# adaLN products in fp32 on four column tiles, and key transposes of 128 columns, in a two-layer hybrid mixer on Trainium2

## The chip, the core and the metric

The kernel runs on one core of a Trainium2 chip. The metric is the device time of one execution, in microseconds (us). The core's engines are called by their names or by the profile's: TensorE (PE; its weight loads are PEld), VectorE (DVE), ScalarE (ACT), GpSimd (POOL), SyncE (SP, whose queue issues most of the DMAs). Each engine works through its own instructions in order.

## What is computed

Two layers, each one mixer with post-normalisation, over 2048 latent tokens (`x`) and 256 context tokens (`ctx`) of width 1024:

```python
shift, scale, gate = split(silu(c) @ w_ada + b_ada, 3)        # (1024) @ (1024 x 3072), per layer
shift_c, scale_c, gate_c = split(silu(c_ctx) @ w_ada + b_ada, 3)
z  = (x  * (1 + scale)   + shift)   @ w_in                    # 1024 x 2560
zc = (xc * (1 + scale_c) + shift_c) @ w_in
# z is cut into: gated MLP over chunks of 128 tokens, grouped-query attention
# (8 heads, 2 key heads, RMS norm and rotary), bidirectional RG-LRU
y = concat(mix_a * silu(a_g), attn * silu(b_g), lru * silu(r_g)) @ w_o
x_new = layer_norm(alpha * x + gate * y)
```

The change touches the first two lines (called adaLN below) and the way in which the keys are laid out for the attention's scores.

## The kernel before

Most products are made in fp16 pairs: a float32 operand is scaled and written as a high part and a low part (the rest), and three products hh, hl, lh are summed in PSUM. The program has a start (`ada_start`, L96), and then for each layer a projection stage (`z_phase`, L299) and an attention stage (`att_phase`, L826).

*The start.* `ada_start` makes shift and scale of layer 0, for both `c` and `ctx` (two rows). The 1024 x 2048 columns of `w_ada` come in 16 chunks of 128 x 1024 (`wada`, six buffers, L113). `split` (L133) turns each into `wadh` on ScalarE (L137) and `wadl` on VectorE (L138). The stationary operand is `vs`, 128 x 4: the high and low parts of silu(c) and silu(c_ctx). Four products per chunk (L157, L158, 512 columns each) add into `acc`, which has four rows: high and low parts. `row` (L123) scales them and adds the bias, and `turn` (L127) turns them with eight float32 products with `sel`, which also adds high and low, into columns `adaT`. The order of TensorE, SyncE, ScalarE and VectorE is as written there.

*The rest of adaLN.* Gate of layer 0, and gate, scale and shift of layer 1, are made by a generator, `ada_rest` (L333), beside layer 0's projections, from the second token block on. An item is one chunk of 128 x 512: a load into `wga` (a buffer of the tag `xm`, which `prep` uses as well), the conversion on ScalarE (L384) and VectorE (L385) into the single buffer `wgh`, and at the next visit two products into `gtp` (L376, L377; `gtp` is one of four buffers of the tag `zps`, which the projections use too). After eight items the row is scaled and added to the bias (L379); `fin` (L351) then either turns it (`gtr`, L355) or adds its halves with a product (`gsu`, L359) and stores the gate to DRAM (L361). `pump(rest, 1)` visits the generator once in each section of 24 products: in `nat` at k = 4 (L537), 512 columns each, and in `conv_in` at k = 4 (L686), 256 columns each. A full block of 256 tokens has eight `nat` and four `conv_in` sections, so 12 visits.

*The projections.* `z_phase` goes over nine blocks (L799). In each, the sections rx, rg, ag, kv, uv, bg run in this order (L807). Generators for normalisation and heads (`heads`, L582), gated MLP (`gmlp`), recurrence (`lru`) and the next block's transposes (`prep`) are advanced by `tick` between the sections. Only TensorE's order is written out here (L782); the other engines' instructions are put in order by the framework, and each engine then works in that order.

*The keys.* `heads` gets the reciprocal roots `rs` with a GpSimd power (L588), scales the heads on VectorE (L596), and writes `kc`, 128 tokens x (high, high, low) x 64 per key head (L624, L625). Four transposes follow per 128 tokens: for each of two key heads one of 128 columns (high, high; L641) and one of 64 (low; L642). ScalarE copies them to `KK` (L643) and `KB` (L644, its first 64 rows). The query transposes `qp` (L648), eight per 128 tokens, are all of 128 columns.

*The attention.* Scores, exponentials and values go in a fixed order on all engines but SyncE (L1284).

## Time and profile before

| | |
|---|---|
| runs | 2929.77, 2930.40, 2931.66 us, median 2930.4 us |
| the profiled execution | 2929.47 us, its span (first to last instruction) 2927.7 us |
| PE busy | 2734.7 us, 93% of the span |
| DVE, ACT, POOL busy | 70%, 48%, 61% |
| mean granted TensorE clock | 0.979 |

Busy time of PE is the union of its matmuls, whose ends are modelled, so the space between the starts of neighbours is the better measure of what one costs. The last column of a timeline row tells how long the engine stood idle before the instruction and which instruction released it. Stages: the start to about 37 us, layer 0's projections to about 700 us, its attention to about 1500 us, and the same for layer 1 behind.

### The profile page before, as it was taken

To read this page: it belongs to the slowest core of one execution; us is meant where nothing else is said; L and a number is where in the kernel's file an instruction comes from. 1 tells how busy PE (TensorE), PEld (TensorE's weight loads), DVE (VectorE), ACT (ScalarE), POOL (GpSimd) and SP (SyncE) were. 2 spreads that over 40 slices of the span, in tenths; PEclk is the share of its full clock that TensorE was granted. 3 is DMA by queue.
4 is the path that set the end of the run, shared out by engine and by line. 5 is a ranking of instruction groups with operands and counts; after the bars stand their busy time and mean duration, and the time that the engine had idled before them with its cause. 6 is when DMAs were issued, how large, how long until landed. Compare 5 with 4: busy or idle time off the path is not lost. (4 is left out here: it accounts for less than half of the span.)

```text
span 2927.7 us, 60696 instructions
## 1 busy us (share of the span) xinstructions
PE 2734.7 (93%) x23931; PEld 1821.0 (62%) x23931; DVE 2062.4 (70%) x4102; ACT 1402.3 (48%) x2594; POOL 1784.0 (61%) x1821
## 2 busy tenths in 40 slices
PE   7999999989799999999999899998988999999998
PEld 3544444546677777677765555564566777777775
DVE  7666565567988777777877555554798877777775
ACT  5444444536554445445542454444465544544452
POOL 3233333356888877677764244433498877887775
PEclk9999999999999999999999999999999999999999
DMA  8222222105421110212114111111433210111001
GB/s 289 85 92 93 86 92 78 53 28 178 131 77 58 56 41 27 69 37 70 52 34 158 52 56 54 50 64 38 140 105 99 70 47 24 49 48 42 26 27 44
DMA packets 118254, 213.60 MB, mean 73 GB/s; under 512 B 13872, under 2 KB 45428, under 8 KB 117968
## 3 DMA queue, kind: packets, MB, share of 16 engines
q1 hardware_dynamic: 115620, 208.84, 21.2%
q8 instruction: 187, 3.06, 0.4%
q10 hardware_dynamic: 2348, 0.89, 0.1%
q14 instruction: 99, 0.81, 0.1%
HBM read 147.54 MB, written 62.14 MB: 72 GB/s over the span
## 5 line engine op out<-in xcount | busy, mean ns | idle before, releaser
L1070 POOL TENSOR_TENSOR Pl<-P 128x512 f16<-128x512 f32 x1131 | 1223.4, 1100 | 329.4 <-ACT P L1063 322.0
L1063 ACT ACTIVATE P<-stp 128x512 f32<-128x512 f32 x1160 | 693.1, 598 | 781.6 <-PE stp L1060 701.0
L978 DVE TENSOR_REDUCE pm<-sps 128x1 f32<-128x256 f32 (+1 forms) x1276 | 750.6, 626 | 270.3 <-PE sps L976 267.6
L1060 PE MATMUL stp<-aQB,KB 65*128 65x256 f16 x2320 | 580.0, 275 | 1.6 <-ACT aQB L991 1.6
L1059 PE MATMUL stp<-aQS,KK 128*128 128x256 f16 x2320 | 577.3, 274 | 0.0
L1087 PE MATMUL pv<-VX,P 128*128 128x129 f16 x4640 | 561.1, 220 | 0.0
L1089 PE MATMUL pv<-VX,Pl 128*128 128x65 f16 x4640 | 529.1, 193 | 6.1 <-POOL Pl L1070 3.1
L976 PE MATMUL sps<-KK,aQS 128*128 128x256 f16 (+1 forms) x1276 | 457.7, 360 | 60.1 <-DVE pm L978 57.4
L1089 PEld LDWEIGHTS <-Pl 128*128 128x128 f16 x4640 | 416.9, 98 | 99.8 <-POOL Pl L1070 5.1
L1087 PEld LDWEIGHTS <-P 128*128 128x128 bf16 x4640 | 431.4, 98 | 64.6 <-issue 49.8
L1060 PEld LDWEIGHTS <-KB 65*128 65x128 f16 x2320 | 227.8, 98 | 91.2 <-issue 0.5
L1059 PEld LDWEIGHTS <-KK 128*128 128x128 f16 x2320 | 230.1, 99 | 83.2 <-issue 13.9
L520 POOL TENSOR_SCALAR xh<-xm 128x512 f16<-128x512 f32 x68 | 46.5, 683 | 276.1 <-ACT xm L517 275.4
L531 PEld LDWEIGHTS <-xh 128*128 128x128 f16 x1040 | 103.1, 99 | 152.7 <-issue 50.8
L533 PEld LDWEIGHTS <-xl 128*128 128x128 f16 x1040 | 103.1, 99 | 125.1 <-issue 7.2
L532 PEld LDWEIGHTS <-xh 128*128 128x128 f16 x1040 | 103.0, 99 | 108.6 <-issue 5.9
L682 PE MATMUL cps<-xh,wh_cc 128*128 128x256 f16 x528 | 147.7, 280 | 4.1 <-POOL xh L520 4.1
L683 PE MATMUL cps<-xl,wh_cc 128*128 128x256 f16 x528 | 147.4, 279 | 3.1 <-DVE xl L521 3.1
L684 PE MATMUL cps<-xh,wl_cc 128*128 128x256 f16 x528 | 147.3, 279 | 1.7 <-DVE wl_cc L185 1.7
L433 POOL TENSOR_SCALAR gt<-gt,sp 128x256 f32<-128x256 f32 x72 | 44.1, 622 | 159.9 <-ACT gt L430 153.9
L976 PEld LDWEIGHTS <-aQS 128*128 128x128 f16 x1276 | 124.8, 98 | 9.7 <-DVE yB L1110 0.4
L755 ACT ACTIVATE uv<-uv 128x512 f32<-128x512 f32 x34 | 21.4, 630 | 204.4 <-DVE uv L754 204.4
(284 smaller groups left out, 5581.4 us busy)
## 6 DMA issues: line engine op xcount, KB each, us to landing
wf<-in_w_in_dram SPq DMA_DIRECT2D x64, 256.0 KB
wga<-in_w_ada_dram SPq DMA_DIRECT2D x64, 256.0 KB
lr<-LRd SPq DMA_DIRECT2D x32, 512.0 KB
SBd<-sbg SPq DMA_DIRECT2D x34, 256.0 KB
QSd<-QS SPq DMA_DIRECT2D x17, 512.0 KB
LRd<-gt SPq DMA_DIRECT2D x34, 256.0 KB
aQS<-QSd SPq DMA_DIRECT2D x17, 512.0 KB
asb<-SBd SPq DMA_DIRECT2D x17, 512.0 KB
```

What stands on the lines that cost most here:

```text
L531: T.matmul(ps[:, :w], xh[:, k, ts], wh[:, k, c0:], start=(k == 0), stop=False)
L682: T.matmul(ps, wh[:, k, cs], xh[:, k], start=(k == 0), stop=False)
L683: T.matmul(ps, wh[:, k, cs], xl[:, k], start=False, stop=False)
L684: T.matmul(ps, wl[:, k, cs], xh[:, k], start=False, stop=(k == KC - 1))
L976: T.matmul(ps[:, :w], QS[:, h, t * 128:(t + 1) * 128], KK[:, kv].rearrange("p a b -> p (a b)")[:, k0:k0 + w], start=True, stop=True)
L978: V.tensor_reduce(pm[:, i:i + 1], ps[:, :w], axis=AX, op=OP.max)
L1059: T.matmul(ps[:, i], KK[:, kv, kt], QS[:, h], start=True, stop=False)
L1060: T.matmul(ps[:, i], KB[:, kv, kt], QB[:, h], start=False, stop=True)
L1063: S.activation(P, ps, AF.Exp)
L1070: less_busy(0.6, 1.04, 2.0).tensor_tensor(Pl, P, Ph, op=OP.subtract)
L1087: T.matmul(pv[:, t, 0:129], Ph[:, i, ts], VX[:, kt, kv, 0:129], start=first, stop=False, skip_group_check=True)
L1089: T.matmul(pv[:, t, 64:129], Pl[:, i, ts], VX[:, kt, kv, 64:129], start=False, stop=end, skip_group_check=True)
```

## The change

`vs` becomes float32, 128 x 2. In the start, the products are made in float32 from the loaded chunk itself. The accumulator is 128 x 256: column group g of 256 goes to rows 32g and 32g + 1, so that each of the four products per chunk sits on column tile g of the array. A product of zeros opens each accumulation. The bias is added by one operation over all 128 rows, and the turning takes rows 32g, 32g + 1 with columns of the identity. `wada` has eight buffers.

In `ada_rest`, the items are chunks of 128 x 1024 (32 in place of 64), with one buffer `wga` of their own and no conversion. The generator yields four times per item, `nat` visits it at k = 1 and k = 5, and `conv_in` at k = 4 as before. Gates are stored from rows 32g, four stores each; `gsu` is gone.

In `heads`, `kc` is laid out (low, high, high), and the second transpose of a key head takes (low, high), 128 columns; `KB` still takes the first 64 rows.

```diff
--- before.py
+++ after.py
@@ -69,8 +69,7 @@
     idF = cst.tile([128, 128], F32, name="idF")
     idH = cst.tile([128, 128], F16, name="idH")
     nhalf = cst.tile([128, 32], F32, name="nhalf")
-    vs = cst.tile([128, KC, 4], F16, name="vs")
-    sel = cst.tile([4, 2], F32, name="sel")
+    vs = cst.tile([128, KC, 2], F32, name="vs")
     adaT = [[cst.tile([128, KC, 2], F32, name=f"adaT{l}{j}") for j in range(2)] for l in range(DEPTH)]
     gate_d = [dr.tile([2, D], F32, name=f"gate_d{l}") for l in range(DEPTH)]
     x1_d = dr.tile([SEQ, D], F32, name="x1_d")
@@ -100,73 +99,47 @@
             nc.scalar.dma_start(craw[8:16], c_ctx.rearrange("(k p) -> k p", p=128))
             bts = []
             for j in range(2):
-                bt = p.tile([4, D], F32, name=f"bt{j}")
+                bt = p.tile([128, 256], F32, name=f"bt{j}")
                 V.memset(bt, 0.0)
-                nc.scalar.dma_start(bt[0:2], rows_bcast(b_ada[0, j * D:(j + 1) * D], D, 2))
+                for g in range(4):
+                    c0 = j * D + g * 256
+                    nc.scalar.dma_start(bt[32 * g:32 * g + 2], rows_bcast(b_ada[0, c0:c0 + 256], 256, 2))
                 bts.append(bt)
             iot = p.tile([128, 128], I32, name="iot")
             G.iota(iot, pattern=[[1, 128]], base=0, channel_multiplier=-1)
             V.tensor_scalar(idF, iot, 0.0, None, op0=OP.is_equal)
-            V.tensor_tensor(sel, idF[0:4, 0:2], idF[0:4, 2:4], op=OP.add)
-            ws, tps = [], []
+            zer = p.tile([128, 256], F16, name="zer")
+            V.memset(zer, 0.0)
+            ws = []
 
             def load():
                 j, k = len(ws) // KC, len(ws) % KC
-                ws.append(p.tile([128, D], F32, name="wada", tag="wada", bufs=6))
+                ws.append(p.tile([128, D], F32, name="wada", tag="wada", bufs=8))
                 nc.sync.dma_start(ws[-1], w_ada[0, k * 128:(k + 1) * 128, j * D:(j + 1) * D])
 
-            for _ in range(6):
+            for _ in range(8):
                 load()
-            accs = [pp.tile([4, 2, 512], F32, name=f"acc{j}") for j in range(2)]
-            rows = [bt.rearrange("p (a b) -> p a b", b=512) for bt in bts]
-
-            def row(j, n):
-                V.scalar_tensor_tensor(rows[j][:, n], accs[j][:, n], 1.0 / (CS * WS), rows[j][:, n],
-                                       op0=OP.mult, op1=OP.add)
-
-            def turn(j):
-                tp = pp.tile([128, KC, 2], F32, name=f"tp{j}")
-                for k in range(KC):
-                    T.matmul(tp[:, k], rows[j][:, k // 4, k % 4 * 128:(k % 4 + 1) * 128], sel, start=True, stop=True)
-                tps.append(tp)
-
-            def split(i):
-                w = ws[i].rearrange("p (a b) -> p a b", b=512)
-                wh = p.tile([128, 2, 512], F16, name="wadh", tag="wadh", bufs=3)
-                wl = p.tile([128, 2, 512], F16, name="wadl", tag="wadl", bufs=3)
-                S.activation(wh, w, AF.Copy, scale=WS)
-                V.scalar_tensor_tensor(wl, w, WS, wh, op0=OP.mult, op1=OP.subtract)
-                if len(ws) < 2 * KC:
-                    load()
-                return wh, wl
-
-            parts = [split(0)]
             S.activation(craw, craw, AF.Silu)
             cps = pp.tile([128, 2, KC], F32, name="cps")
             T.transpose(cps.rearrange("p i k -> p (i k)"), craw, idF[:16, :16])
-            vcs = p.tile([128, KC, 2], F32, name="vcs")
-            V.tensor_copy(vcs, cps.rearrange("p i k -> p k i"))
-            V.tensor_scalar(vs[:, :, 0:2], vcs, CS, None, op0=OP.mult)
-            V.scalar_tensor_tensor(vs[:, :, 2:4], vcs, CS, vs[:, :, 0:2], op0=OP.mult, op1=OP.subtract)
-            for i in range(2 * KC):
-                j, k = i // KC, i % KC
-                if i + 1 < 2 * KC:
-                    parts.append(split(i + 1))
-                wh, wl = parts.pop(0)
-                for n in range(2):
-                    T.matmul(accs[j][:, n], vs[:, k], wh[:, n], start=(k == 0), stop=False)
-                    T.matmul(accs[j][:, n], vs[:, k], wl[:, n], start=False, stop=(k == KC - 1))
-                if i == KC + 1:
-                    row(0, 0)
-                    row(0, 1)
-                if i == KC + 3:
-                    turn(0)
-                if i == KC + 5:
-                    V.tensor_scalar(adaT[0][0], tps[0], 0.0, None, op0=OP.add)
-            row(1, 0)
-            row(1, 1)
-            turn(1)
-            V.tensor_scalar(adaT[0][1], tps[1], 1.0, None, op0=OP.add)
+            V.tensor_copy(vs, cps.rearrange("p i k -> p k i"))
+            tps = []
+            for j in range(2):
+                acc = pp.tile([128, 256], F32, name=f"acc{j}")
+                T.matmul(acc, zer[:, 0:128], zer, start=True, stop=False, skip_group_check=True)
+                for k in range(KC):
+                    w = ws[j * KC + k]
+                    for g in range(4):
+                        T.matmul(acc[32 * g:32 * g + 2], vs[:, k], w[:, g * 256:(g + 1) * 256], start=False,
+                                 stop=(k == KC - 1), skip_group_check=True)
+                    if len(ws) < 2 * KC:
+                        load()
+                V.tensor_tensor(bts[j], acc, bts[j], op=OP.add)
+                tp = pp.tile([128, KC, 2], F32, name=f"tp{j}")
+                for k in range(KC):
+                    T.matmul(tp[:, k], bts[j][:, k % 2 * 128:(k % 2 + 1) * 128],
+                             idF[:, 32 * (k // 2):32 * (k // 2) + 2], start=True, stop=True)
+                V.tensor_scalar(adaT[0][j], tp, float(j), None, op0=OP.add)
 
     GRP = {"uv": (0, 512), "ag": (512, 512), "kv": (1024, 512), "bg": (1536, 512), "cc": (2048, 512)}
 
@@ -305,7 +278,7 @@
             def pop(i):
                 return st.enter_context(tc.tile_pool(name=f"zps{l}_{i}", bufs=1, space=PSUM, reuse_waits="tile"))
 
-            zp = Router(op, ["wh_ag wl_ag wh_kv wl_kv wh_uv wl_uv", "xn xm xh xl wgh grow",
+            zp = Router(op, ["wh_ag wl_ag wh_kv wl_kv wh_uv wl_uv", "xn xm xh xl wga grow",
                              "rx qk t1 t2 kc qc QS rp ct sn uv vhl ss rs rt mv s6 rv rsq2 sag sbg zm",
                              "wh_bg wl_bg gt0 gt1 lra th xr xrh xrl hc"])
             pp = Router(pop, ["zc", "tr", "zps"])
@@ -331,63 +304,54 @@
                 return early.pop(0)
 
             def ada_rest():
-                items = [(l2, j, h, k) for l2, j in [(0, 2)] + [(a, b) for a in range(1, DEPTH) for b in (2, 1, 0)]
-                         for h in range(2) for k in range(KC)]
-                ws, parts, acc, row, fins = [], [], None, None, None
+                items = [(l2, j, k) for l2, j in [(0, 2)] + [(a, b) for a in range(1, DEPTH) for b in (2, 1, 0)]
+                         for k in range(KC)]
+                zer = MZ[1][:, 0, 0:1].to_broadcast([128, 128])
+                mov = MZ[2][:, 0:1, 0:64].to_broadcast([128, 4, 64])
+                ws, acc, row, fins = [], None, None, None
 
                 def ld(i):
-                    l2, j, h, k = items[i]
-                    ws.append(zp.tile([128, 512], F32, name="wga", tag="xm", bufs=2))
-                    c0 = j * D + h * 512
-                    nc.sync.dma_start(ws[-1], w_ada[l2, k * 128:(k + 1) * 128, c0:c0 + 512])
-
-                def bias(l2, j, h):
-                    row = zp.tile([4, 512], F32, name="grow", tag="grow")
-                    V.memset(row, 0.0)
-                    c0 = j * D + h * 512
-                    nc.sync.dma_start(row[0:2], rows_bcast(b_ada[l2, c0:c0 + 512], 512, 2))
-                    return row
-
-                def fin(l2, j, h, row):
+                    l2, j, k = items[i]
+                    ws.append(zp.tile([128, D], F32, name="wga", tag="wga"))
+                    nc.sync.dma_start(ws[-1], w_ada[l2, k * 128:(k + 1) * 128, j * D:(j + 1) * D])
+
+                def fin(l2, j, row):
                     if j < 2:
-                        tp = pp.tile([128, 4, 2], F32, name="gtr", tag="tr", bufs=2)
-                        for k in range(4):
-                            T.matmul(tp[:, k], row[:, k * 128:(k + 1) * 128], sel, start=True, stop=True)
-                        V.tensor_scalar(adaT[l2][j][:, 4 * h:4 * h + 4], tp, float(j), None, op0=OP.add)
+                        tp = pp.tile([128, KC, 2], F32, name="gtr", tag="tr", bufs=2)
+                        for k in range(KC):
+                            T.matmul(tp[:, k], row[:, k % 2 * 128:(k % 2 + 1) * 128],
+                                     idF[:, 32 * (k // 2):32 * (k // 2) + 2], start=True, stop=True)
+                        V.tensor_scalar(adaT[l2][j], tp, float(j), None, op0=OP.add)
                     else:
-                        ps = pp.tile([2, 512], F32, name="gsu", tag="tr", bufs=2)
-                        T.matmul(ps, sel, row, start=True, stop=True)
-                        V.tensor_copy(row[0:2], ps)
-                        nc.sync.dma_start(gate_d[l2][:, h * 512:(h + 1) * 512], row[0:2])
+                        for g in range(4):
+                            nc.sync.dma_start(gate_d[l2][:, g * 256:(g + 1) * 256], row[32 * g:32 * g + 2])
 
                 ld(0)
                 yield
-                for i in range(len(items) + 1):
+                yield
+                for i, (l2, j, k) in enumerate(items):
+                    if k == 0:
+                        acc = pp.tile([128, 256], F32, name="gtp", tag="zps", bufs=4)
+                        T.matmul(acc, zer, mov, start=True, stop=False, skip_group_check=True)
+                        row = zp.tile([128, 256], F32, name="grow", tag="grow")
+                        G.memset(row, 0.0)
+                        for g in range(4):
+                            c0 = j * D + g * 256
+                            nc.sync.dma_start(row[32 * g:32 * g + 2], rows_bcast(b_ada[l2, c0:c0 + 256], 256, 2))
+                    w = ws.pop(0)
+                    for g in range(4):
+                        T.matmul(acc[32 * g:32 * g + 2], vs[:, k], w[:, g * 256:(g + 1) * 256], start=False,
+                                 stop=(k == KC - 1), skip_group_check=True)
+                    if i + 1 < len(items):
+                        ld(i + 1)
+                    if k == KC - 1:
+                        V.tensor_tensor(row, acc, row, op=OP.add)
+                        fins = l2, j, row
+                    for _ in range(4):
+                        yield
                     if fins:
                         fin(*fins)
                         fins = None
-                    if i:
-                        l2, j, h, k = items[i - 1]
-                        w = parts.pop(0)
-                        if k == 0:
-                            acc = pp.tile([4, 512], F32, name="gtp", tag="zps", bufs=4)
-                        if k == 2:
-                            row = bias(l2, j, h)
-                        T.matmul(acc, vs[:, k], w[:, 0], start=(k == 0), stop=False)
-                        T.matmul(acc, vs[:, k], w[:, 1], start=False, stop=(k == KC - 1))
-                        if k == KC - 1:
-                            V.scalar_tensor_tensor(row, acc, 1.0 / (CS * WS), row, op0=OP.mult, op1=OP.add)
-                            fins = l2, j, h, row
-                    if i < len(items):
-                        w = zp.tile([128, 2, 512], F16, name="wgh", tag="wgh")
-                        f = ws.pop(0)
-                        S.activation(w[:, 0], f, AF.Copy, scale=WS)
-                        V.scalar_tensor_tensor(w[:, 1], f, WS, w[:, 0], op0=OP.mult, op1=OP.subtract)
-                        parts.append(w)
-                        if i + 1 < len(items):
-                            ld(i + 1)
-                    yield
-                fin(*fins)
 
             W = Wt[l]
 
@@ -533,7 +497,7 @@
                     T.matmul(ps[:, :w], xl[:, k, ts], wh[:, k, c0:], start=False, stop=(k == KC - 1))
                     if t:
                         pump(fm, 1)
-                    if k == 4:
+                    if k % 4 == 1:
                         pump(rest, 1)
                 return ps
 
@@ -621,8 +585,8 @@
                                                 snv[:, None, :, s].to_broadcast([128, w, 2, 16]), op=OP.mult)
                         V.tensor_tensor(t1, t1, t2, op=OP.add)
                     kc = zp.tile([128, 2, 3, 64], F16, name="kc", tag="kc", bufs=2)
-                    V.tensor_copy(kc[:, :, 0:2], t1[:, 8:10, None].to_broadcast([128, 2, 2, 64]))
-                    V.tensor_tensor(kc[:, :, 2], t1[:, 8:10], kc[:, :, 0], op=OP.subtract)
+                    V.tensor_copy(kc[:, :, 1:3], t1[:, 8:10, None].to_broadcast([128, 2, 2, 64]))
+                    V.tensor_tensor(kc[:, :, 0], t1[:, 8:10], kc[:, :, 1], op=OP.subtract)
                     kcs.append(kc)
                     if full(b):
                         qc = zp.tile([128, 8, 2, 64], F16, name="qc", tag="qc", bufs=2)
@@ -638,8 +602,8 @@
                     kc = kcs[t]
                     kp = pp.tile([128, 2, 2, 128], F16, name="kp", tag="tr", bufs=2)
                     for j in range(2):
-                        T.transpose(kp[:, 0, j], kc[:, j, 0:2].rearrange("p a b -> p (a b)"), idH)
-                        T.transpose(kp[0:64, 1, j], kc[:, j, 2], idH)
+                        T.transpose(kp[:, 0, j], kc[:, j, 1:3].rearrange("p a b -> p (a b)"), idH)
+                        T.transpose(kp[:, 1, j], kc[:, j, 0:2].rearrange("p a b -> p (a b)"), idH)
                     S.copy(KK[:, :, kt], kp[:, 0])
                     S.copy(KB[0:64, :, kt], kp[0:64, 1])
                     if full(b):
```

## Rows read from the trace of the kernel before

**Rows 1.** Stages: window, us, busy us (instructions) of PE, PEld, DVE, ACT, POOL, clock, DMA share, GB/s
```profile
37.00:100.00 63.00, 56.08 (x306) 31.11 (x305) 55.03 (x113) 26.92 (x54) 27.74 (x30) 0.95 0.53 178
100.00:515.00 415.00, 391.38 (x2242) 203.97 (x2243) 242.38 (x445) 198.48 (x361) 140.18 (x161) 0.97 0.27 89
```

**Rows 2.** Waits of PE, 100 to 515 us: total us, times, longest
```profile
PE gtp L377 <- DVE wgh L385: 22.9, 6, 5.0
```

**Rows 3.** Timeline, 156 to 170 us: start, us, engine, line, operation, idle before and releaser
```profile
156.04 3.83 POOL L588 TENSOR_TENSOR rs<-rt,nhalf 128x20 f32<-128x20 f32 x1
...
163.26 0.80 DVE L385 SCALAR_TENSOR_TENSOR wgh<-wga,wgh 128x512 f16<-128x512 f32 x1
164.12 0.58 PE L377 MATMUL gtp<-wgh,vs 128*4 128x512 f16 x1 [5.01 <-DVE wgh L385]
...
169.30 0.43 PE L533 MATMUL zps<-wh_bg,xl 128*128 128x512 f16 x1
169.57 0.38 PE L531 MATMUL zps<-wh_bg,xh 128*128 128x512 f16 x1
169.79 0.38 PE L532 MATMUL zps<-wl_bg,xh 128*128 128x512 f16 x1
```

**Rows 4.** Groups by line and shape, PE: 100 to 515 us, then 1500 to 1760 us (busy us, mean ns)
```profile
L531 PE MATMUL zps<-wh_uv,xh 128*128 128x512 f16 x80 | 32.9, 411 | 0.0
...
L531 PE MATMUL zps<-wh_uv,xh 128*128 128x512 f16 x32 | 12.1, 379 | 0.0
```

**Rows 5.** Timeline of PE around one pair of `gtp` products
```profile
185.23 0.27 PE L683 MATMUL cps<-xl,wh_cc 128*128 128x256 f16 x1
185.34 0.27 PE L684 MATMUL cps<-xh,wl_cc 128*128 128x256 f16 x1
185.54 0.38 PE L376 MATMUL gtp<-wgh,vs 128*4 128x512 f16 x1
185.75 0.38 PE L377 MATMUL gtp<-wgh,vs 128*4 128x512 f16 x1
186.06 0.28 PE L682 MATMUL cps<-xh,wh_cc 128*128 128x256 f16 x1
```

**Rows 6.** Timeline of PE around `gsu`
```profile
171.95 0.38 PE L533 MATMUL zps<-wh_bg,xl 128*128 128x512 f16 x1
172.25 1.01 PE L359 MATMUL gsu<-grow,sel 4*2 4x512 f32 x2
173.20 0.38 PE L376 MATMUL gtp<-wgh,vs 128*4 128x512 f16 x1
```

**Rows 7.** Timeline of PE, 10 to 37 us
```profile
10.25 0.59 PE L157 MATMUL acc<-wadh,vs 128*4 128x512 f16 x1 [1.56 <-DVE vs L150]
...
15.75 0.41 PE L158 MATMUL acc<-wadl,vs 128*4 128x512 f16 x1
...
29.44 0.58 PE L157 MATMUL acc<-wadh,vs 128*4 128x512 f16 x1
...
35.08 1.94 PE L130 MATMUL tp<-sel,bt 4*128 4x2 f32 x16 [0.34 <-DVE bt L124]
```

**Rows 8.** Waits of SyncE's queue, 100 to 515 us: total us, times, longest
```profile
SPq L342 <- DVE xl L521: 47.0, 19, 7.4
```

**Rows 9.** Timeline of PE around the key and query transposes
```profile
175.76 0.22 PE L641 MATMUL kp<-idH,kc 128*128 128x128 f16 x1
175.91 0.24 PE L642 MATMUL kp<-idH,kc 128*64 128x128 f16 x1
...
176.42 0.62 PE L648 MATMUL qp<-idH,qc 128*128 128x128 f16 x8
```

**Rows 10.** Timeline of ACT in the start stage
```profile
24.70 1.06 ACT L137 ACTIVATE wadh<-wada 128x1024 f16<-128x1024 f32 x1 [0.22 <-DMA wada<-in_w_ada_dram]
25.97 1.06 ACT L137 ACTIVATE wadh<-wada 128x1024 f16<-128x1024 f32 x1 [0.21 <-DMA wada<-in_w_ada_dram]
```

**Rows 11.** Tile `gsu`, its weight loads: duration ns min, median, max
```profile
L359 PEld LDWEIGHTS gsu<-grow,sel x8: 75/76/78, 172.3 to 322.4; 4*2 4x2 f32 x8
```

## The prediction

> **What bounds the kernel now.** The table by stage comes first. Between 100 and 515 us, the part of layer 0's projections in which `ada_rest` is worked off, TensorE is busy for 391.4 of 415 us while VectorE has 242.4 [rows 1]. So there a microsecond of TensorE is a microsecond of the span. The order of TensorE's work is fixed by hand and the attention behind it starts when that list is through, so what is saved here should last to the end. The waits of TensorE in that stage come next: of the 23.6 us in which it is idle, 22.9 are one group, the second `gtp` product waiting for L385, six times [rows 2]. The timeline around one of them tells why: GpSimd's `rs` takes 3.83 us, VectorE stands in order behind it, L385 is late, and TensorE stops 5.01 us in the middle of a pair of products [rows 3]. After it TensorE runs at its lower clock level (1.2 of 2.4 GHz): from 164.12 to 169.30 the 512-column products make twelve steps of 0.43 us, behind that the step is 0.22 us again [rows 3]. That is 12 x 0.21 = 2.5 us more. Four of the six waits are followed by such a stretch, which shows in the mean of L531 on `uv`, 411 ns against 379 ns in layer 1, where nothing of `ada_rest` runs [rows 4]. Waits and their after-effect together are 22.9 + 10 = 33 us.
>
> **What falls away in `ada_rest`.** The 64 conversions on ScalarE and the 64 on VectorE cost TensorE nothing themselves; their price is the 33 us above. Then 64 pairs of products: from L684 at 185.34 to L682 at 186.06 are 0.72 us where the plain step is 0.11, so a pair costs 0.61 us: twice 0.215, and 0.09 each for going into and out of the narrow products [rows 5]. 64 x 0.61 = 39.0 us. The four `gsu` products go too: from L533 at 171.95 to the next `gtp` at 173.20 are 1.25 us, less L533's own step of 0.22 is 1.03 us [rows 6], times four 4.1 us. Sum 43.1 us.
>
> **What comes in `ada_rest`.** 32 chunks of four fp32 products with 256 columns. The `gsu` row shows what fp32 is: one product is two instructions of 512 columns, and of the 1.03 us some 0.18 for going in and out leave 0.43 us for each [rows 6]. 256 columns are then 0.213 us, eight pieces per chunk. No row shows two column tiles at work, so whether they overlap has to be bounded. One after another: 8 x 0.213 + 2 x 0.09 = 1.89 us. All four tiles beside each other: 2 x 0.213 + 0.18 = 0.61 us. Between them lies what the issue order alone gives: a tile's second piece must follow its first, the next tile's first piece can start with that second piece, and so eight pieces fill five steps, 5 x 0.213 + 0.18 = 1.25 us. I take 1.25, which is also the middle of the ends; 32 x 1.25 = 40 us, and four zeroing products of 0.11 us (an L684 step [rows 5]). Against 43.1 us that is -2.7 us (serial +17.8, beside each other -23.2). The turns stay as they are: two of 16 instructions for four of 8, 1.94 us per 16 [rows 7].
>
> **The stalls.** Nothing on VectorE or ScalarE stands before the new products, so the 33 us should go. What is late next: `kp` needs VectorE's `kc`, and the fourth `zps` buffer is still held by `gtp`. In layer 1 the same sections without `ada_rest` run at 379 ns [rows 4], so I let only 4 us come back: -29 us.
>
> **New waits.** There is one `wga` buffer, so a chunk's load is issued only after the products of the chunk before, and 512 KB in place of 256 KB. Four visits lie between: two sections of 24 products at 0.215 us, or four of 24 at 0.109 [rows 5], 10.3 to 10.5 us. SyncE stood up to 7.4 us at `xl` before such a load [rows 8]; behind it queue `xn` loads and stores. The 16 bias loads (8 before) wait for a GpSimd memset that stands in POOL's queue, and the next chunk is behind them on SyncE. The eight gate stores replace four. I take +3 us, between 0 and 12. Visits: 130 at 20 per block instead of 66 at 12, so it lasts 6.5 blocks of eight; nothing in layer 0's projections waits for it.
>
> **The key transposes.** Two 128-wide and two 64-wide products take 0.66 us from 175.76 to 176.42. The eight full ones behind them take 0.62 us, less the 0.22 of one that is seven steps of 0.057 [rows 9]; all wide, four are 0.23. Saving 0.43 us, 36 times (18 tiles of 128 tokens in two layers): 15.5 us over both layers. Some fall where TensorE waits anyway: -14 us, between 0 and -15.5.
>
> **The start.** Before, the first chunk's product starts at 10.25 and the last turn at 35.08, 1.94 us long; 5.5 us of it, until 15.75, run at the lower level, and again after the first turn from 29.44 for 3.4 us [rows 7]. New: start about 9.9 (two VectorE steps fewer), 16 x 1.25 = 20, lost to the clock 2.75 + 1.7, each turn with its addition 2.5 (its 1.94 and some 0.55 for the addition, for which the last turn waited idle 0.34 us [rows 7]): 39.4 us against 37.0. The first turn now stands ahead of the second half's products on TensorE, which wait behind its addition; that is in the 2.5. Behind it, the `cc` weights no longer queue behind the conversions on VectorE, and the stage to 100 us has 63.0 - 56.1 = 6.9 us of idle TensorE [rows 1]; I count 2 us of that back: +0.4 us. The shorter bias rows and their six more loads hide behind the wait for the first chunk.
>
> **Sum.** -2.7 - 29 + 3 - 14 + 0.4 = -42.3 us. The profiled execution took 2929.5 us (span 2927.7), the median of the runs is 2930.4; so 2888.
>
> **Rivals.**
> *Serial tiles.* The change does not do what it says: 1.89 us per chunk. +17.8 in `ada_rest`, the start ends at 9.9 + 30.2 + 9.5 = 49.6 us, +12.6 - 2; sum 17.8 - 29 + 3 - 14 + 10.6 = -11.6: 2918. For it: every product in the trace takes its turn. Against it: nothing but habit; no narrow product had a neighbour on other columns.
> *Full overlap.* 0.61 us per chunk; the start is then held by the loads, which feed a conversion each 1.27 us [rows 10], and gains some 5 us. -23.2 - 29 + 3 - 14 - 5 = -68: 2861. Against it: order of issue within a tile. The Trainium skill (TensorE: Matmul & The Clock Gate, Part 3: Packing small matmuls) gives starts some 4 ns apart for products on different tiles, in strict order; no run here shows it.
> *The stall moves.* With L385 gone, TensorE arrives earlier at `kp` or at a `zps` buffer and waits for the same `rs` there: 29 us come back, 2917. For it: `rs` is as long as before. Against it: layer 1.
> *Pieces that pay each time.* Slower: each of the eight pieces pays its own weight load, 0.076 us [rows 11], and a switch of 0.09: 8 x 0.379 = 3.03 us. 32 x 3.03 + 0.4 - 43.1 = +54.3; the start ends at 9.9 + 48.5 + 9.5 = 68 us, +31 less the 6.9 of idle time; with -29, +3 and -14 that is +38: 2968. It decides from 2.13 us per chunk: with c for that price, the sum is 32c + 0.4 - 43.1 in `ada_rest`, 16c - 19.65 at the start and -40 for the rest, 48c - 102.3 in all. For it: `gsu` and `gtp` pay on entering. Against it: within a pair the second product follows after 0.21 us with its load hidden [rows 5]. The Trainium skill has a rule on its side: in the same page, under What overlaps and what doesn't, weight loads pass a running product only on other rows of the array, and four column tiles share all rows. By it alone (loads bare, no switches) a chunk is 2.5 us and the time about 2943, an estimate; the pair shows a hidden load, on one tile. Under Key Properties in TensorEngine Tiling (Array Packing) only a change of mode drains the engine, not one of tile, which the 0.09 us at the ends of a pair agree with.
>
> **How the numbers follow.** Forecast 0.42, serial 0.24, full overlap 0.10, moved stall 0.12, paying pieces 0.12. A change under 0.2% (5.9 us) can hardly be told from none by a measurement of this kernel. The range runs from just under full overlap, 2858, to above the two cases at 2917 and 2918 with their bounds, 2930: it leaves out the paying pieces and some edges. Faster: forecast and overlap whole, seven tenths of the two middle cases: 0.77. Within 0.2%: 0.09. Slower: 0.14, the paying pieces and what spills over.
>
> **What would show it.** Right: the second `gtp` group's waits for VectorE gone, `uv` products at 379 ns in layer 0, `kp` four times in 0.23 us, a chunk from entry to exit 1.25 us with the start of each tile's first piece together with the second of the one before. Serial: eight starts 0.21 us apart. Wrong: TensorE waiting for `wga` loads at many chunks, a start stage that ends past 45 us, or the 5 us stops standing at `kp` or `zps`.

## The result, and the profile of the kernel after

The changed kernel takes **2899.6 us** (median of 4 runs, 2895.9 to 2901.4); the kernel before took 2931.0 us beside it (4 runs, 2929.8 to 2935.9). The ratio is 0.9888, with a 95% interval from 0.9871 to 0.9905: 31.4 us faster, where 42 were forecast. The profiled execution took 2900.0 us (span 2897.9), 29.5 us less than the profiled execution before. The ledger below compares the two traces and so is made against that figure.

The profile's first part (busy time, share of the span, instructions) and the table by stage of the kernel after, with the columns of [rows 1]:

```profile
PE 2699.2 (93%) x24121; PEld 1818.4 (63%) x24121; DVE 1995.7 (69%) x4000; ACT 1342.6 (46%) x2513; POOL 1778.6 (61%) x1825
```

```profile
37.00:100.00 63.00, 55.67 (x287) 28.96 (x286) 55.46 (x112) 24.37 (x49) 27.04 (x29) 0.89 0.57 187
100.00:515.00 415.00, 394.42 (x2529) 220.89 (x2530) 215.56 (x405) 176.79 (x328) 159.18 (x188) 0.98 0.27 89
...
110.00:560.80 450.80, 426.38 (x2750) 241.89 (x2748) 229.77 (x434) 192.64 (x358) 165.76 (x197) 0.98 0.27 88
```

The second row is where one would look for the vanished waits, and it seems to say that little happened: TensorE is busy for 394.4 of 415 us, where it was 391.4. VectorE and ScalarE are the engines that lost load, 242.4 to 215.6 us and 198.5 to 176.8. A window of fixed length hides that more work went through it. The third row therefore runs from one piece of work to another: from the last product of the first `rx` group of 24 in the second block (110.0) to the same product in the ninth block (560.8). Before, the same pieces start at 111.7 and 595.2:

```profile
111.70:595.20 483.50, 454.34 (x2626) 241.26 (x2624) 279.95 (x514) 231.91 (x421) 167.40 (x194) 0.97 0.25 83
```

The stretch is 32.7 us shorter. TensorE's busy time fell by 28.0 us and its idle time only by 4.7, from 29.2 to 24.4. That is the result in one line: **the products became cheaper, the waits hardly fewer.** The forecast had it the other way round.

Landmarks along the whole run (start of the same TensorE product in both traces, us) show where the gain comes and that it stays. For an `rx` row it is the last product of the section's first group of 24, for the `rg` row the last product of the section:

```
landmark                               before    after    difference
last turn of the start                   35.1     30.3      -4.7
first transpose of the projections       37.0     32.2      -4.8
first block, rg                          58.9     54.6      -4.3
second block, rx                        111.7    110.0      -1.7
third block, rx                         186.9    175.0     -11.9
fifth block, rx                         337.0    303.2     -33.8
seventh block, rx                       487.1    450.0     -37.2
ninth block, rx                         595.2    560.8     -34.4
layer 0 attention, first mp             696.3    662.7     -33.6
layer 1, first rx                      1559.1   1526.3     -32.7
layer 1 attention, first mp            2109.3   2075.8     -33.4
layer 1 attention, mp number 256       2796.0   2765.8     -30.2
```

**The four tiles.** One chunk of the new `ada_rest` between `zps` products (start, us, engine, line, operation, count; the first `gtp` row is the answer for a window that ends at 193.20, the second that for one ending at 193.70):

```profile
192.77 0.38 PE L497 MATMUL zps<-wh_ag,xl 128*128 128x512 f16 x1
193.08 0.40 PE L343 MATMUL gtp<-wga,vs 128*2 128x256 f32 x4
...
193.08 0.61 PE L343 MATMUL gtp<-wga,vs 128*2 128x256 f32 x8
193.63 0.39 PE L495 MATMUL zps<-wh_ag,xh 128*128 128x512 f16 x1
```

Four of the eight pieces start inside 0.12 us, in fact at 193.080, .087, .094 and .100, 7 ns apart. The other four start 0.215 us later, at 193.295, .302, .309 and .315. The next plain product comes at 193.63. From L497 to L495 are 0.86 us, less L497's own step of 0.22 is 0.64 us for a chunk, where a pair of half-precision products took 0.61 [rows 5]. The bound for full overlap was 0.61, the value taken 1.25. Which piece belongs to which tile the profile doesn't tell; that four start within 0.02 us of one another, and that the next product isn't held up for it, it does.

The weight loads of this chunk in the timeline (start, us, count), those of all chunks (min/median/max ns), and the `uv` products that answer to [rows 4] (busy us, mean ns):

```profile
193.08 0.11 PEld L343 LDWEIGHTS gtp<-wga,vs 128*2 128x2 f32 x8 [0.42 <-issue]
...
L343 PEld LDWEIGHTS gtp<-wga,vs x240: 80/82/85, 115.5 to 507.7; 128*2 128x2 f32 x120
...
L495 PE MATMUL zps<-wh_uv,xh 128*128 128x512 f16 x96 | 36.5, 380 | 0.0
```

Each piece has a load of 0.08 us, and eight of those one after another would fill the whole 0.64 us. The first line shows them done together in 0.11 us: beside one another, and beside the first pieces, which start at the same time. The Trainium skill (TensorE: Matmul & The Clock Gate, Part 3, Measured speedup vs the span model) gives some 4 ns from tile to tile; this trace shows 7 ns. The same part of the Trainium skill, under What overlaps and what doesn't, lets a weight load pass a running product only on another row group; this trace disagrees, since four column tiles share all rows and the eight loads end 0.11 us after the first piece started. The `uv` products are back at 380 ns from 411, as in layer 1: the stretches at the lower clock behind waits became short there.

**The waits.** TensorE's waits between 110 and 560 us (total us, times, longest), in place of [rows 2]:

```profile
PE gtp L343 <- DMA wga<-in_w_ada_dram: 7.1, 3, 3.3
PE zps L495 <- DVE uv L720: 6.1, 5, 1.2
PE gtr L322 <- ACT KB L608: 4.7, 1, 4.7
PE cps L646 <- POOL xh L484: 3.0, 1, 3.0
PE qp L612 <- DVE qc L594: 2.3, 6, 0.4
PE kp L606 <- DVE kc L589: 0.6, 1, 0.6
```

The group of 22.9 us is gone. Six smaller ones stand in its place, 23.8 us together, where all groups of the same stretch before sum to 29.1. Two have causes that can be read. The first is the queue that issues the loads. SyncE's largest group of waits (total, times, longest), and its queue around the longest of the three stops:

```profile
SPq L730 <- DVE sbg L729: 78.3, 11, 11.9
```

```profile
374.62 0.33 SPq L730 DMA_DIRECT2D SBd<-sbg  x1
375.05 0.37 SPq L316 DMA_DIRECT2D wga<-in_w_ada_dram  x1
```

TensorE around the same load:

```profile
363.86 0.61 PE L343 MATMUL gtp<-wga,vs 128*2 128x256 f32 x8
...
379.95 1.03 PE L343 MATMUL gtp<-wga,vs 128*2 128x256 f32 x8 [3.27 <-DMA wga<-in_w_ada_dram]
```

The buffer was free when the chunk of 363.86 was through, but its load was issued at 375.05, directly behind a store of `sbg` that SyncE had stood waiting to issue. The other two late loads (306.78 and 517.66) stand directly behind the same store too. The chunk that wants the load waits 3.27 us, and then runs at the lower clock: 1.03 us in place of 0.61.

The second cause is VectorE's order of work. VectorE ahead of one of the five `uv` waits:

```profile
501.63 0.82 DVE L589 TENSOR_TENSOR kc<-t,kc 128x128 f16<-128x128 f32 x1
502.37 0.80 DVE L594 TENSOR_TENSOR qc<-t,qc 128x512 f16<-128x512 f32 x1
503.28 1.15 DVE L578 TENSOR_TENSOR t<-qk,ct 128x512 f32<-128x512 f32 x2
504.36 0.68 DVE L720 SCALAR_TENSOR_TENSOR uv<-uv,zps 128x512 f32<-128x512 f32 x1
```

The instruction for which the next `zps` product waits (L720) stands behind the heads' work (L589, L594, L578), and TensorE stops 1.23 us for it. Before, L385 was delayed by the heads too: by their `rs` on GpSimd and by what VectorE did behind it [rows 3].

**The key transposes.** Layer 1, where nothing of `ada_rest` runs:

```profile
1732.72 0.22 PE L605 MATMUL kp<-idH,kc 128*128 128x128 f16 x1
1734.13 0.23 PE L606 MATMUL kp<-idH,kc 128*128 128x128 f16 x1 [1.19 <-DVE kc L589]
1734.20 0.22 PE L605 MATMUL kp<-idH,kc 128*128 128x128 f16 x1
1734.26 0.22 PE L606 MATMUL kp<-idH,kc 128*128 128x128 f16 x1
1734.86 0.62 PE L612 MATMUL qp<-idH,qc 128*128 128x128 f16 x8 [0.39 <-DVE qc L594]
```

The same place in the trace of the kernel before:

```profile
1766.89 0.24 PE L642 MATMUL kp<-idH,kc 128*64 128x128 f16 x1 [1.22 <-DVE kc L625]
```

The steps of 0.06 us are there, where they were 0.15 to 0.17. The wait of 1.19 us for VectorE's `kc` stood there before (1.22). New is the wait behind the four: the query transposes now wait 0.39 us for `qc`. From the first `kp` to the first `qp` are 2.14 us; before it was 2.17 (1765.45 to 1767.62). What the transposes save is waited for in the next instruction.

**The start.** TensorE from 8 to 74 us, against [rows 7]:

```profile
8.33 2.74 PE L133 MATMUL acc<-wada,vs 128*2 128x256 f32 x24
...
12.38 1.03 PE L133 MATMUL acc<-wada,vs 128*2 128x256 f32 x8 [1.31 <-DMA wada<-in_w_ada_dram]
...
30.34 1.95 PE L140 MATMUL tp<-idF,bt 128*128 128x2 f32 x16 [0.55 <-DVE bt L137]
32.15 1.07 PE L478 MATMUL tr<-idF,xn 128*128 128x128 f32 x8
...
73.92 0.30 PE L478 MATMUL tr<-idF,xn 128*128 128x128 f32 x1 [2.36 <-DMA xn<-in_x_dram]
```

The start no longer depends on the products: TensorE waits for the loads of `wada` (3.7 us in six waits), even at the lower clock, where a chunk takes 1.03 us. It is through 4.8 us earlier, and 4.3 of it are still there at `rg`. Then TensorE waits 2.36 us for the second block's `xn`, which before came in time; at the second block's `rx` 1.7 us are left. The clock has no part in that loss: between the two landmarks it was 0.97 in both traces (59 to 109 us before, 55 to 107 after). What pulls the stage from 37 to 100 us down to 0.89, against 0.95 [rows 1], lies ahead of that, with 0.70 from 32 to 55 us.

### The profile page after: what moved, and what is told of

It is laid out like the page before. It is cut to its first block, busy times and chain, and to the rows that moved or that the text cites. A ratio compares the mean times of both kernels' runs of the same rounds, so it can differ in the third digit from the quotient of the medians.

```text
span 2897.9 us, 60732 instructions
## 1 busy us (share of the span) xinstructions
PE 2699.2 (93%) x24121; PEld 1818.4 (63%) x24121; DVE 1995.7 (69%) x4000; ACT 1342.6 (46%) x2513; POOL 1778.6 (61%) x1825
## 5 line engine op out<-in xcount | busy, mean ns | idle before, releaser
L495 PEld LDWEIGHTS <-xh 128*128 128x128 f16 x1040 | 102.4, 98 | 124.5 <-issue 19.0
L497 PEld LDWEIGHTS <-xl 128*128 128x128 f16 x1040 | 102.3, 98 | 122.7 <-issue 2.9
L496 PEld LDWEIGHTS <-xh 128*128 128x128 f16 x1040 | 102.3, 98 | 115.4 <-issue 9.2
```

The lines of the kernel that those rows point to most:

```text
L495: T.matmul(ps[:, :w], xh[:, k, ts], wh[:, k, c0:], start=(k == 0), stop=False)
```

## The experiments

Ten kernels, each timed beside the kernel before (medians of 2932 to 2933 us). They come in the order of the questions.

### Do the four tiles run beside each other, and what is that worth?

All four products of a chunk are sent to the same column tile, at the start and in `ada_rest`, so that their sums run into one another. The rest is as in the changed kernel.

```diff
-    T.matmul(acc[32 * g:32 * g + 2], vs[:, k], w[:, g * 256:(g + 1) * 256], start=False,
+    T.matmul(acc[0:2], vs[:, k], w[:, g * 256:(g + 1) * 256], start=False,
```

> The changed kernel with the four products of a chunk all on column tile 0; their sums run into one another, so that adaLN's values are others. Theory (the four column tiles work beside each other): a chunk in the projections goes from 0.64 us to 8 x 0.213 + 0.18 = 1.89 us, 32 x 1.25 = 40 us, and the start ends 10 to 18 us later, of which some is hidden behind loads; in all 40 to 55 us slower than the changed kernel, slower than the kernel before too. Rival (pieces are paced by their weight loads of 0.08 us and not by the columns): still 0.64 us per chunk, and within 5 us of the changed kernel.

Measured: 2938.5 us (10 runs), ratio to the kernel before 1.0023 [1.0013, 1.0033]: 39 us slower than with four tiles, just under the lower end expected. The timeline of one of its chunks:

```profile
135.19 0.38 PE L497 MATMUL zps<-wh_ag,xl 128*128 128x512 f16 x1
135.50 1.89 PE L343 MATMUL gtp<-wga,vs 128*2 128x256 f32 x8
137.32 0.39 PE L495 MATMUL zps<-wh_ag,xh 128*128 128x512 f16 x1
```

By the same reading as above a chunk costs 137.32 - 135.19 - 0.22 = 1.91 us; its eight starts are 0.216 us apart. The bound for serial work was 1.89. So the column tiles make the gain: 32 chunks times 1.27 us are 41 us, and 5.8 us more are left of the slower start at the second block; 39 of these 47 reach the end. Without the tiles the change would have been a small loss. Going into and out of the narrow products is in both figures: 1.91 us less eight steps of 0.216 leaves 0.18, 0.64 less two of 0.215 leaves 0.21.

### Which part of the change carries the time?

First the key transposes alone, put into the kernel before:

```diff
-    V.tensor_copy(kc[:, :, 0:2], t1[:, 8:10, None].to_broadcast([128, 2, 2, 64]))
-    V.tensor_tensor(kc[:, :, 2], t1[:, 8:10], kc[:, :, 0], op=OP.subtract)
+    V.tensor_copy(kc[:, :, 1:3], t1[:, 8:10, None].to_broadcast([128, 2, 2, 64]))
+    V.tensor_tensor(kc[:, :, 0], t1[:, 8:10], kc[:, :, 1], op=OP.subtract)
...
-    T.transpose(kp[0:64, 1, j], kc[:, j, 2], idH)
+    T.transpose(kp[:, 1, j], kc[:, j, 0:2].rearrange("p a b -> p (a b)"), idH)
```

> The kernel before with the key transposes of 128 columns alone. Theory (the saved steps are waited for again, because TensorE then stands at VectorE's kc and qc): within 3 us of the kernel before, and in layer 1 the waits of kp and qp for VectorE grow by what the transposes save. Rival (the term of the prediction holds alone, and something else ate it in the changed kernel): 14 us faster, between 10 and 15.5.

Measured: 2930.6 us (12 runs), ratio 0.9994 [0.9984, 1.0004], nothing that can be told from no change. Of its theory, the time came out, and in layer 1 the waits grew before `qp`, but hardly before `kp`. Its timeline there is that of the changed kernel:

```profile
1766.63 0.23 PE L642 MATMUL kp<-idH,kc 128*128 128x128 f16 x1 [1.19 <-DVE kc L625]
...
1767.36 0.62 PE L648 MATMUL qp<-idH,qc 128*128 128x128 f16 x8 [0.39 <-DVE qc L630]
```

Then the new start alone, in the kernel before (with a copy of the condition vector in single precision for it, and the two half-precision parts made from that copy for the old `ada_rest`):

```diff
+    vf = cst.tile([128, KC, 2], F32, name="vf")
...
-                    T.matmul(accs[j][:, n], vs[:, k], wh[:, n], start=(k == 0), stop=False)
-                    T.matmul(accs[j][:, n], vs[:, k], wl[:, n], start=False, stop=(k == KC - 1))
+                        T.matmul(acc[32 * g:32 * g + 2], vf[:, k], w[:, g * 256:(g + 1) * 256], start=False,
+                                 stop=(k == KC - 1), skip_group_check=True)
```

> The kernel before with the new start alone; the rest of adaLN as before from fp16 parts. Theory (what the start gains is given back when TensorE stands at the load of x and runs at the lower clock level): the first transposes of the projections some 4 to 5 us earlier, the second block's rx section no more than 2 us earlier, the time within 3 us of the kernel before. Rival (the start's gain lasts, and the rest lost it): 4 to 5 us faster.

Measured: 2931.4 us (12 runs), ratio 0.9999 [0.9989, 1.0009]. In its trace the first block's `rg` comes 3.2 us earlier and the second block's `rx` 0.8 us. And the changed kernel with the old start in place of the new one:

```diff
-                        T.matmul(acc[32 * g:32 * g + 2], vs[:, k], w[:, g * 256:(g + 1) * 256], start=False,
-                                 stop=(k == KC - 1), skip_group_check=True)
+                    T.matmul(accs[j][:, n], vh[:, k], wh[:, n], start=(k == 0), stop=False)
+                    T.matmul(accs[j][:, n], vh[:, k], wl[:, n], start=False, stop=(k == KC - 1))
```

> The changed kernel with the old start. Theory: as fast as the changed kernel within 3 us, some 31 us under the kernel before, since all that lasts comes from the rest of adaLN beside layer 0's projections. Rival: 4 to 5 us slower than the changed kernel, the start's share.

Measured: 2899.7 us (5 runs), ratio 0.9889 [0.9873, 0.9905], the time of the whole change. Neither the transposes nor the start are worth anything alone, and without the new start nothing is lost, so the gain is put down to `ada_rest`. `ada_rest` without the new transposes was not run.

### Why are the waits still there?

L385, the conversion for which TensorE waited, is taken out of the kernel before; both products of a pair read the high part, so the low part of the weights is left out of `ada_rest`. No other work changes.

```diff
-    T.matmul(acc, vs[:, k], w[:, 1], start=False, stop=(k == KC - 1))
+    T.matmul(acc, vs[:, k], w[:, 0], start=False, stop=(k == KC - 1))
...
-    V.scalar_tensor_tensor(w[:, 1], f, WS, w[:, 0], op0=OP.mult, op1=OP.subtract)
```

> The kernel before without L385: the low part of the rest of adaLN's weights is left out and both products of a pair read the high part, so TensorE has the same products and VectorE nothing of them. It prices the stalls alone. Theory (the 33 us of waits and slow clock fall away, but TensorE then arrives earlier at VectorE's uv, kc and qc and about half comes back; the changed kernel has 36 us over the six blocks, of which the cheaper products are 22): 14 us faster than the kernel before, between 9 and 19, with new waits of zps and qp for VectorE. Rival (the prediction's term): 29 us faster.

Measured: 2929.1 us (11 runs), ratio 0.9987 [0.9978, 0.9996]: 4 us. Both theories miss, and this is the clearest run of the study: the wait that the prediction valued at 33 us with its after-effect is taken away, and 4 us come of it. The three largest groups of TensorE's waits from 100 to 560 us in this kernel:

```profile
PE gsu L359 <- DVE grow L379: 11.4, 2, 6.0
PE gtr L355 <- DVE grow L379: 5.4, 1, 5.4
PE gtp L376 <- ACT wgh L384: 4.0, 3, 2.8
```

The 22.9 us have become 20.8 in front of other instructions of the same pass, mostly for VectorE's `grow`. VectorE ahead of the longest of these waits:

```profile
157.66 1.56 DVE L595 TENSOR_TENSOR qk<-qk,rs 128x640 f32<-128x640 f32 x2 [2.80 <-POOL rs L587]
...
168.13 0.67 DVE L379 SCALAR_TENSOR_TENSOR grow<-gtp,grow 4x512 f32<-4x512 f32 x1
```

VectorE still stands for the heads' `rs`, here 2.80 us, and then works through the heads before it comes to what TensorE asked for; what waits for it is whoever asks next. Whether a shorter `rs` on GpSimd would free these waits is a rival that no run tries.

If it is the neighbourhood of one section that matters, moving the visits should help. In the kernel before, `ada_rest` is not visited in the `uv` sections:

```diff
-                    if k == 4:
+                    if k == 4 and g != "uv":
                         pump(rest, 1)
```

> The kernel before, but the rest of adaLN is not visited in the two uv sections of a block (10 visits in place of 12), all products as before. VectorE works off the heads while TensorE is in uv. Theory (the stops belong to the place: whatever TensorE asks of VectorE while VectorE is at the heads is late, be it L385 or the finished row): most of the 22.9 us of waits and the slow clock behind them go without any change to the products, 15 to 28 us faster than the kernel before. Rival (VectorE is the bound of the stage, and the next thing it owes is waited for instead): waits for uv, kc or qc in their place, less than 8 us faster.

Measured: 2940.3 us (10 runs), ratio 1.0029 [1.0019, 1.0039], slower: neither theory nor rival has the time, but the waits for `uv` came that the rival names. The four largest groups of TensorE's waits from 100 to 600 us:

```profile
PE gtp L377 <- DVE wgh L385: 8.2, 5, 4.0
PE qp L648 <- DVE grow L360: 7.4, 1, 7.4
PE zps L531 <- DVE uv L756: 6.6, 3, 4.2
PE qp L648 <- DVE adaT L356: 6.5, 1, 6.5
```

The wait at `gtp` shrinks from 22.9 to 8.2 us, and 20.5 stand before `qp` and `zps`, all for VectorE. The other way round, in the changed kernel, the heads' transposes are asked for one tick later:

```diff
                 yield
+                yield
                 for t in range(2):
```

> The changed kernel with the key and query transposes one tick, a section of some 5 us, later. Theory (the 0.43 us saved per 128 tokens are waited for at VectorE's kc and qc, and those are late by less than a section): these waits vanish in layer 1, some 1.6 us of waits and the lower clock behind them per block, 8 to 17 us faster than the changed kernel over both layers. Rival (VectorE's whole chain is the bound there, uv comes next): the waits of zps for uv grow by the same, within 3 us of the changed kernel.

Measured: 2895.9 us (4 runs), ratio 0.9880 [0.9863, 0.9896], 3.7 us under the change (2.3 by the ratios), with intervals that overlap. The 8 to 17 us of the theory did not come. Its trace shows no wait for `kc` or `qc` between 100 and 560 us; instead these two groups stand in it (the first from 100 to 560 us, the second from 1480 to 2060 us; L721 is the changed kernel's L720):

```profile
PE zps L495 <- DVE uv L721: 13.7, 5, 3.2
...
PE ga L528 <- POOL vhl L520: 11.7, 4, 2.9
```

In all three kernels the waits changed their places and went on. Between the same two products as above (the second and the ninth block's `rx`) TensorE is idle for 28 us without L385, 38 with the visits moved and 28 with the later transposes, beside 29 before and 24 after the change. Shown is that removing or moving one waiter frees little. That the order of work on VectorE sets the pace is what the releasers in these rows say; which of its instructions would have to become shorter was not tried.

### What does the queue of the loads cost?

The loads of `wga` are issued from ScalarE's queue in place of SyncE's:

```diff
-    nc.sync.dma_start(ws[-1], w_ada[l2, k * 128:(k + 1) * 128, j * D:(j + 1) * D])
+    nc.scalar.dma_start(ws[-1], w_ada[l2, k * 128:(k + 1) * 128, j * D:(j + 1) * D])
```

> The changed kernel with the chunk loads of the rest of adaLN issued from ScalarE's queue. Theory (SyncE stands at other stores, up to 11.9 us at SBd, while a chunk's load waits behind): TensorE's 7 us of waits for wga and the slow clock behind them go, 5 to 12 us faster than the changed kernel. Rival (ScalarE in its turn stands at the products that free the buffer, and TensorE waits for ScalarE's copies): no faster, or slower by up to 10 us.

Measured: **2891.0 us** (2889.5 to 2893.0, 4 runs), ratio 0.9860 [0.9846, 0.9873], 8.6 us under the change (8.2 by the ratios). No run of the one reaches into the runs of the other; the two intervals just overlap, from 0.9871 to 0.9873. The three largest groups of waits from 100 to 560 us, and the load behind the same chunk as above on ScalarE's queue:

```profile
PE qp L612 <- DVE qc L594: 4.7, 6, 0.8
PE zps L495 <- DVE uv L720: 4.3, 2, 2.2
PE gtr L322 <- ACT KB L608: 3.2, 1, 3.2
```

```profile
367.16 0.33 ACTq L316 DMA_DIRECT2D wga<-in_w_ada_dram  x1
```

No wait for `wga` is left, and the load of that chunk is not held: it goes out 3.0 us after the products of the chunk before began (364.14 in this trace), where it was 11.2 us. The idle time between the second and the ninth block's `rx` falls from 24.4 to 17.9 us, about the 7.1 that stood before `wga`; the other waits are as long as they were, so it was these loads, and not others behind them on SyncE, that gave the time, as far as TensorE's waits tell. This is the fastest version found. The later transposes added to it:

```diff
-    nc.sync.dma_start(ws[-1], w_ada[l2, k * 128:(k + 1) * 128, j * D:(j + 1) * D])
+    nc.scalar.dma_start(ws[-1], w_ada[l2, k * 128:(k + 1) * 128, j * D:(j + 1) * D])
...
                 yield
+                yield
```

> Both: chunk loads from ScalarE's queue and transposes one tick later. If both theories hold, the sum of the two gains, 13 to 29 us faster than the changed kernel; if either falls, what the other gives alone.

Measured: 2897.3 us (2894.9 to 2900.2), ratio 0.9881 [0.9867, 0.9895]. The two gains don't add; together they are no better than the later transposes alone.

### Can the gain of the start be kept?

In the changed kernel the second block's `x` loads, for which TensorE waits 2.36 us, go to ScalarE's queue:

```diff
-    nc.sync.dma_start(xt, src[t * 128:(t + 1) * 128, h * 512:(h + 1) * 512])
+    (nc.scalar if l == 0 and b == 1 else nc.sync).dma_start(xt, src[t * 128:(t + 1) * 128, h * 512:(h + 1) * 512])
```

> The changed kernel with the loads of x for the second block issued from ScalarE's queue. Theory (the earlier start is given back because TensorE reaches the second block's transposes before their x, which SyncE issues behind the weights): the 2.4 us wait for xn and the slow clock behind it go, some 4 us faster than the changed kernel. Rival (the conversions of the weights are next in line, or ScalarE's queue is as late): the second block's rx section starts no earlier, within 2 us of the changed kernel.

Measured: 2901.1 us (2899.1 to 2904.1), ratio 0.9894 [0.9881, 0.9907], no gain. The wait for `xn` is gone and `uv` starts 2.8 us earlier, but behind it (37 to 105 us) stands

```profile
PE qp L612 <- DVE wsl L228: 4.7, 1, 4.7
```

which was 1.6 us in the changed kernel: the weights of the next section are still being split on VectorE. The second block's `rx` comes at 113.5, later than the 110.0 of the changed kernel. That the gain of the start can't be kept at all is not shown; this way doesn't keep it.

## Why the prediction was right in size and wrong in its terms

The time fell inside the range and the sign was the forecast's, but two large errors worked against each other, and that they nearly met was luck. The terms, against the traces:

```
term                          predicted     shown
ada_rest's products              -2.7       -22
stalls and new waits            -29 +3      about -8.5
key transposes                  -14         about -1
start                            +0.4        -1.7
sum                             -42         about -33 at the attention of layer 1
```

**"I take 1.25"** (the price of a chunk) is the term that was mis-sized first. Measured: 0.64 us, within 0.03 of the bound for full overlap. The argument for 1.25 was that a tile's second piece follows its first and the next tile's first piece can start with it. The trace shows first all four tiles' first pieces, 7 ns apart, and then all four second ones. So 32 x 0.64 = 20.5, with the four zeroing products (0.11 us each) 20.9, against 43.1 us that fell away: -22 where -2.7 stood. The price of what fell away, 0.61 per pair and 1.03 per `gsu`, is not contradicted by anything. The rival that had the mechanism, full overlap, was given one chance in ten, against an order of issue that no row showed; that 1.25 is also the middle of two bounds is no evidence either.

**"The stalls: -29"** is the step that failed outright. The waits for L385 did go, and the `uv` products did come back to 380 ns, as the prediction said one would see. But the idle time of the stretch fell by 4.7 us only (24.4 against 29.2). The lower clock cost some 9.6 us before (43 products of 512 columns at 0.21 us more, 5 of 256 at 0.1) and some 5.8 after (10 and 37), so it gave back 3.8. Together 8.5 us, not 26. The reason given against the rival *the stall moves* was layer 1, in which the sections run at 379 ns without `ada_rest`. That row told of the products' clock and not of the waits: layer 1 of the kernel before has its own, as the 1.22 us at `kc` show. The runs with L385 taken out (-4 us), with the visits moved (+8 us) and with the transposes moved all show nearly as much idle time or more, at other places.

**"New waits: +3"** was too low in its first item alone: `wga` costs 7.1 us of waits, and moving its loads gave 8 to 9. The mechanism was the one that the prediction gave, loads held behind SyncE's other work, but the size was read from the old loads' wait of up to 7.4 us [rows 8]. What held the three late loads was the store of `sbg`, each time directly ahead of them on SyncE. SyncE stood at it for up to 11.9 us; in the kernel before it was 4.1 at most, so that trace did not show the size at this store.

**"The key transposes: -14"** failed for the same reason as the stalls. Each saves its 0.43 us or nearly, and hardly any of it lasts, because TensorE is ahead of the other engines at that place. In layer 1's projections, between the same two products (1559.1 to 2109.3 us before, 1526.3 to 2075.8 after), the `kp` steps sum to 6.2 us less and TensorE's idle time to 6.0 us more, 4.0 of them before `qp`, for VectorE and for ScalarE's copies. The prediction set only 1.5 us aside for that. Alone the part is worth 0.9994 [0.9984, 1.0004]; in the changed kernel the projections of layer 1 gain under 1 us.

**"The start: +0.4"** ended close for a reason that it did not have. The chunks were not 20 us of products: the loads set the pace, the start ends at 32.2 us and not at 39.4, and 5 us were gained as in the rival of full overlap. But 3 of them were gone by the second block's `rx`.

That the errors were linked can be seen from the prediction's own formula, 48c - 102.3: with the measured c = 0.64 it gives -71.6 us, a time of 2859, 41 us too fast. What c made good, the two terms that count a wait's end as a gain (stalls and transposes, -43 together) had spent in advance.

About 2 us of the shorter busy time belong to none of the terms in the table. By the steps between starts they are the key transposes of layer 0 (3.6 us less), against longer turns (1.2) and query transposes (0.8). Some 3 us of the lead are lost at the beginning of layer 1's attention (-33.4 to -30.2), where the change touches nothing: the same pieces (2090 to 2250 us before, 2057 to 2220 after) ran at a granted clock of 0.97 before and 0.95 after. Why is left open.

## What to carry to other kernels

Products that write few rows are cheap in single precision if they lie on different column tiles: price a group of four as one, and test the overlap in one run before it is averaged with anything. A wait of the bound engine for an engine that works in order is not a price tag on the instruction it waits for: ask which instruction of that engine is wanted next, and count only what the wait's end makes earlier there. When a load gets larger and its buffers fewer, look at everything on its queue that may stand in front of it, and give it a queue that is not waiting.

## What was not expected of the hardware

- Four column tiles start 7 ns apart, in two rounds 0.215 us apart, and a single-precision chunk of four 256-column products costs 0.64 us with four tiles against 1.91 on one: 3.0 times less, entry and exit included.
- The eight weight loads of a chunk, 0.08 us each on tiles that share all rows, are through 0.11 us after the first starts and cost nothing that the starts show.
- One store for which SyncE waited up to 11.9 us made three of 32 loads behind it late, although some 13 us lie between two chunks; moving the loads to another queue was worth 8 to 9 us of the kernel's time.
